# Column mean of an 8192 x 8192 matrix: the first load in two halves, the early load in mid-stream, the last groups loaded in pairs

## The chip, the cores and the metric

The kernel runs on one core of a Trainium2 chip. The metric is device time in microseconds (us) for one execution; the time shown for a kernel is the median of several runs. A profile is one execution taken by the hardware profiler. Its engines are called PE (TensorE), DVE (VectorE), ACT (ScalarE), POOL (GpSimd) and SP (SyncE, which here issues the loads).

## The reference

```python
def setup_inputs():
    return {"x": np.random.randn(8192, 8192).astype(np.float32)}

def reference(x: np.ndarray) -> np.ndarray:
    return np.mean(x, axis=0)
```

256 MiB of float32 (268.4 MB) are read once, and 8192 column means are written.

## The kernel before

The 8192 rows are cut into 64 groups of 128 rows (G = 64), numbered 0 to 63; one group is 128 partitions x 8192 columns, 4 MB. A block is F = 512 columns, so a group has 16 blocks. The tile `bufs` holds six such groups: four slots for loads (0 to 3), `both` (slot 4) and the accumulator `acc` (slot 5).

*Loads.* All loads are issued by SP, in program order, through `load` (line 76). A load into a slot waits for the VectorE add that last read the slot. `load_rows` loads n adjacent groups at once, with partition p taking n adjacent rows; the sum over rows is the same. The order is: the last two blocks of group 60 into `early` (0.5 MB); groups 0 to 3 in one load of 16 MB; groups 4 and 5 straight into `both` and `acc`; five blocks (9 to 13) of group 63 into `early` (1.25 MB); then from group 6 to group 55 pairs of 8 MB, each into two of the four slots in turn; then single groups 56 to 59, 14 blocks of group 60, groups 61 and 62, and group 63 in four pieces (blocks 4 to 7, 0 to 3, 14 and 15, 8).

*Adds.* `add` (line 96) makes a VectorE addition. Where it waits for a load and for the add before it, a no-op on ScalarE or GpSimd waits for both (line 99) and VectorE waits for the no-op. The first two adds fold groups 0 to 3 and then 4 and 5 in a width of 16384 columns. In the loop every pair costs two adds, `both = a + b` and `acc = acc + both`; the first of them frees the pair's slots. At groups 24 and 32 GpSimd adds parts of `early` into `acc` (line 129), 4 blocks and 3. Groups 56 to 59 cost one add each. Of group 60 VectorE adds blocks 0 to 13, of group 61 blocks 7 to 15. GpSimd adds blocks 14, 15 and 8 of group 62 (line 148).

*The end.* What is left is summed over partitions by TensorE with a matrix whose entries are 1/8192 (line 183), into PSUM tiles `bank` (blocks 0 to 7), `wide` (blocks 9 to 13), `two` (14, 15) and `last` (8). TensorE takes its matmuls in the order in which the list `sums` was filled: blocks 2 to 4 and 0 to 1 of `acc`, blocks 0 to 6 of group 61, blocks 5 to 7 of `acc`, then groups 62 and 63 as they come, with the rest of `acc` between. Each matmul of 512 columns stands in the trace as two. ScalarE copies the four larger results out of PSUM (line 198), VectorE copies the last one (line 214), and SP and ScalarE issue five small stores (line 201).

Everything around the change stands in program order on SP, ScalarE, GpSimd and TensorE; VectorE's adds run in the order written.

Of the kernel before, what the change touches and what calls it, by code (L numbers as in the profile page):

```python
# [9 lines left out]
def kernel(  # L10
# [2 lines left out]
    x: bass.AP,  # L13
    out: bass.AP,
):

    nc = tc.nc
    f32 = mybir.dt.float32
    M, N = x.shape  # L40
    P = nc.NUM_PARTITIONS
    F = 512
    W = F // 4
    G = M // P
# [3 lines left out]
    sb = ctx.enter_context(tc.tile_pool(name="sb", bufs=1))  # L48
    psp = ctx.enter_context(tc.tile_pool(name="psum", bufs=1, space=bass.MemoryType.PSUM))

    bufs = sb.tile([P, U, N], f32, name="bufs")
    both = bufs[:, U - 2, :]
    acc = bufs[:, U - 1, :]
    ones = sb.tile([P, 32], f32, name="ones")
    early = sb.tile([P, 7 * F], f32, name="early")
    tail = sb.tile([P, W], f32, name="tail")
    warm = sb.tile([P, 32], f32, name="warm")
    nc.gpsimd.memset(ones[:], 1.0 / M)  # L58
# [16 lines left out]
    def load(dst, src):  # L75
        ins = tc.keep_in_program_order(nc.sync.dma_start(out=dst, in_=src)).ins  # L76
        k = len(loads)
        over = loads[k - 8:k - 6] if k >= 8 and k % 2 == 0 else []
        tc.declare_no_dep(ins, group="loads", keep=over, reason="the reader of the buffer waited")
        for o in over:  # L80
            tc.add_manual_dep(ins, o.name, sync, reason="covers the next load too")
        tc.add_to_no_dep_group("loads", ins)
        loads.append(ins)
        return ins

    def rows(g, n=1):
        return x[g * P:(g + n) * P, :]

    def load_rows(g, u, n):
        return load(bufs[:, u:u + n, :], rows(g, n).rearrange("(p j) c -> p j c", j=n))  # L90

    adds, joins = [], {}

    def add(dst, a, b, dmas):

        ins = nc.vector.tensor_add(out=dst, in0=a, in1=b).ins  # L96
        if dmas and adds:
            waiter = nc.scalar if len(adds) % 8 > 1 else nc.gpsimd
            nop = joins[waiter] = tc.keep_in_program_order(waiter.nop()).ins  # L99
            for o in dmas + adds[-1:]:  # L100
                tc.add_manual_dep(nop, o.name, sync, reason="the no-op waits")
            for group in ("loads", "adds"):
                tc.declare_no_dep(ins, group=group, reason="the no-op waited")
            tc.add_manual_dep(ins, nop.name, sync, reason="waits for both at once")
        elif adds:
            tc.declare_no_dep(ins, group="loads", reason="the add ahead waited")
        tc.declare_no_dep(ins, group="early", reason="the no-op waited, or the add behind it")
        tc.add_to_no_dep_group("adds", ins)
        adds.append(ins)

    load(early[:, 5 * F:], rows(G - 4)[:, 14 * F:])
    first, second = load_rows(0, 0, 4), load_rows(4, 4, 2)
    load(early[:, :5 * F], rows(G - 1)[:, 9 * F:14 * F])
    add(bufs[:, 2:4, :], bufs[:, 2:4, :], bufs[:, 0:2, :], [first])
    add(bufs[:, 4:6, :], bufs[:, 4:6, :], bufs[:, 2:4, :], [second])
    add(acc, acc, both, [])
    tc.keep_in_program_order(nc.scalar.copy(out=warm[:], in_=ones[:]))  # L117
    ahead = []
    g = 6
    while g < G - 8:  # L120
        u = (g + 2) % 4
        dma = load_rows(g, u, 2)
        add(both, bufs[:, u, :], bufs[:, u + 1, :], [dma])
        add(acc, acc, both, ahead)
        ahead = []
        if g in (24, 32):
            lo, hi = (0, 4) if g == 24 else (4, 7)
            cols = slice((9 + lo) * F, (9 + hi) * F)
            ins = tc.keep_in_program_order(nc.gpsimd.tensor_add(  # L129
                out=acc[:, cols], in0=acc[:, cols], in1=early[:, lo * F:hi * F])).ins  # L130
            tc.add_to_no_dep_group("early", ins)
            ahead = [ins]
        g += 2

    while g < G - 4:
        row = bufs[:, (g + 2) % 4, :]
        add(acc, acc, row, [load(row, rows(g))])
        g += 1
    for lo, hi, loaded in [(0, 14, 14), (7, 16, 16)]:
        row = bufs[:, (g + 2) % 4, :]  # L140
        dma = load(row[:, :loaded * F], rows(g)[:, :loaded * F])
        cols = slice(lo * F, hi * F)
        add(acc[:, cols], acc[:, cols], row[:, cols], [dma])
        g += 1
    r61, r62, r63 = [bufs[:, (g + 1 + j) % 4, :] for j in range(3)]
    load(r62, rows(g))
    for cols in [slice(14 * F, 16 * F), slice(8 * F, 9 * F)]:
        joined = tc.keep_in_program_order(nc.gpsimd.tensor_add(  # L148
# [7 lines left out]
    def blocks(row, lo, hi):  # L156
        for i in range(lo, hi):
            sums.append((banks[i // 4], i % 4, 0, row[:, i * F:(i + 1) * F]))
# [5 lines left out]
                at = lo * F + q * n + c  # L164
                sums.append((dst, q, c, row[:, at:at + min(F, n - c)]))

    blocks(acc, 2, 5)
    blocks(acc, 0, 2)
    blocks(r61, 0, 7)
    blocks(acc, 5, 8)  # L170
    blocks(r62, 0, 8)
    spread(wide, acc, 9, 14, slice(1))
    blocks(r63, 4, 8)
# [83 lines left out]
```

## Time and profile before

| | |
|---|---|
| Median of 3 runs | 628.53 us (628.39 to 628.57) |
| Span of the profiled execution | 626.4 us |
| VectorE busy | 529.3 us (85%), 60 instructions |
| TensorE busy | 13.3 us (2%), 126 matmuls |
| GpSimd busy | 12.0 us (2%) |
| ScalarE busy | 3.7 us (1%) |
| Read from HBM | 268.44 MB, 429 GB/s over the span |

The profiled execution's span is what the engines and queues cover between its first and last instruction; the time of a run also has what lies around it. Times inside the profile are in us from the start of the span. The chain of waits is followed back from the last instruction to what released it; the timeline merges like instructions that follow each other; the groups give the busy time and the mean of one instruction for each line, engine, operation and shape. In the timeline, the bracket behind a group names how long its engine was idle before it and what ended the idle time.

### The profile page before, as it was taken

Reading aid. Unit: us, or ns where it says so; the run is one execution under the profiler, and the core shown is the slowest. Engines: PE = TensorE matmul, PEld = TensorE weight load, DVE = VectorE, ACT = ScalarE, POOL = GpSimd, SP = SyncE. Lnnn points to the kernel's source line nnn. Section 1 sums busy time; section 2 is a strip of 40 time slices with the busy share of each in tenths; the row PEclk is TensorE's granted clock in tenths of the full one; section 3 lists DMA queues with packets and bytes.
Section 4 is the critical chain, followed back from the end, with each engine's and each line's share of the span. In section 5 each row is a group of like instructions: output and inputs, shape, how many; then the busy total and the mean of one; then the engine's idle time right before and its main releaser. Section 6 shows DMA issues by size and latency. Waiting matters only on the chain.

```text
span 626.4 us, 484 instructions
## 1 busy us (share of the span) xinstructions
PE 13.3 (2%) x126; PEld 4.0 (1%) x126; DVE 529.3 (85%) x60; ACT 3.7 (1%) x6; POOL 12.0 (2%) x10
## 2 busy tenths in 40 slices
PE   0000000000000000000000000000000000000008
PEld 0000000000000000000000000000000000000002
DVE  0028999998888998889998899888898888999992
ACT  0000000000000000000000000000000000000001
POOL 0000000000000000020000200000000000000002
PEclk9999999999999999999999999999999999999999
DMA  8999999999999999999999999999999999999997
GB/s 372 465 402 428 459 410 460 402 469 402 469 402 469 402 469 402 469 402 469 402 465 406 439 431 427 444 410 460 402 469 402 469 402 469 402 435 435 419 435 305
DMA packets 5930, 268.50 MB, mean 429 GB/s; under 512 B 660, under 2 KB 668, under 8 KB 1064
## 3 DMA queue, kind: packets, MB, share of 16 engines
q1 hardware_dynamic: 5912, 268.46, 99.3%
q8 instruction: 1, 0.02, 0.0%
q10 hardware_dynamic: 16, 0.01, 0.0%
q14 instruction: 1, 0.01, 0.0%
HBM read 268.44 MB, written 0.03 MB: 429 GB/s over the span
## 4 chain that ended last, share of the span: by engine, by line
DMA 59%; DVE 30%; another core or an unknown queue 10%; issue 0%; SPq 0%; ACTq 0%; PE 0%; POOL 0%; POOLq 0%
DMA bufs<-in_x_dram 59%; DVE bufs L96 30%; SPq L76 0%; ACTq L99 0%; PE last L183 0%; DVE tail L214 0%; POOL ready L61 0%; POOL ones L58 0%; POOLq L99 0%; POOLq L241 0%
## 5 line engine op out<-in xcount | busy, mean ns | idle before, releaser
L96 DVE TENSOR_TENSOR bufs<-bufs 128x8192 f32<-128x8192 f32 (+3 forms) x59 | 529.0, 8966 | 85.9 <-DMA bufs<-in_x_dram 43.0
L183 PE MATMUL bank<-bufs,ones 128*32 128x512 f32 x62 | 10.0, 716 | 610.3 <-DVE bufs L96 610.0
L129 POOL TENSOR_TENSOR bufs<-bufs,early 128x2048 f32<-128x2048 f32 (+1 forms) x2 | 7.9, 3954 | 348.5 <-DVE bufs L96 348.5
L148 POOL TENSOR_TENSOR bufs<-bufs 128x1024 f32<-128x1024 f32 (+1 forms) x2 | 3.6, 1824 | 258.9 <-DMA bufs<-in_x_dram 258.9
L214 DVE COPY tail<-last 128x128 f32<-128x128 f32 x1 | 0.3, 291 | 8.8 <-PE last L183 8.8
L183 PEld LDWEIGHTS bank<-bufs,ones 128*32 128x32 f32 x62 | 2.2, 121 | 616.4 <-issue 614.5
L198 ACT COPY bufs<-bank 128x512 f32<-128x512 f32 x2 | 1.2, 586 | 617.9 <-PE bank L183 617.9
L183 PE MATMUL wide<-bufs,ones 128*32 128x512 f32 (+1 forms) x32 | 2.5, 432 | 0.0
L117 ACT ACT_TABLE_LOAD x1 | 1.3, 1283 | 0.7 <-PEq L241 0.7
L183 PE MATMUL two<-bufs,ones 128*32 128x256 f32 x16 | 1.2, 380 | 0.0
L183 PEld LDWEIGHTS wide<-bufs,ones 128*32 128x32 f32 x32 | 1.0, 110 | 1.8 <-issue 1.8
L183 PE MATMUL last<-bufs,ones 128*32 128x128 f32 x16 | 0.8, 279 | 0.1
L198 ACT COPY bufs<-wide 128x640 f32<-128x640 f32 x1 | 0.7, 692 | 1.1 <-PE wide L183 1.1
L183 PEld LDWEIGHTS last<-bufs,ones 128*32 128x32 f32 x16 | 0.4, 109 | 1.2 <-issue 0.6
L183 PEld LDWEIGHTS two<-bufs,ones 128*32 128x32 f32 x16 | 0.4, 109 | 0.1
L198 ACT COPY bufs<-two 128x256 f32<-128x256 f32 x1 | 0.4, 372 | 0.1
L117 ACT COPY warm<-ones 128x32 f32<-128x32 f32 x1 | 0.2, 217 | 0.0
L61 POOL TENSOR_TENSOR ready<-ones 128x1 f32<-128x1 f32 x1 | 0.2, 193 | 0.1
L58 POOL MEMSET ones<- 128x32 f32 x1 | 0.1, 125 | 0.3 <-POOLq L241 0.3
L241 POOL MEMSET const-float32-0.0<- 128x1 f32 x1 | 0.1, 98 | 0.2 <-issue 0.2
L241 POOL MEMSET const-bfloat16-1.0<- 128x1 bf16 x1 | 0.1, 102 | 0.0
L241 POOL MEMSET const-uint8-127<- 128x1 uint8 x1 | 0.1, 102 | 0.0
(1 smaller groups left out, 0.1 us busy)
## 6 DMA issues: line engine op xcount, KB each, us to landing
bufs<-in_x_dram SPq DMA_DIRECT2D x6, 4096.0 KB, 20.4
bufs<-in_x_dram SPq DMA_DIRECT2D x1, 3584.0 KB
bufs<-in_x_dram SPq DMA_DIRECT2D x2, 1024.0 KB, 18.7
early<-in_x_dram SPq DMA_DIRECT2D x1, 1280.0 KB
early<-in_x_dram SPq DMA_DIRECT2D x1, 512.0 KB
bufs<-in_x_dram SPq DMA_DIRECT2D x1, 512.0 KB, 19.4
bufs<-in_x_dram SPq DMA_DIRECT2D x27, 29.9
bufs<-in_x_dram SPq DMA_DIRECT2D x1, 256.0 KB, 19.7
```

Source lines behind the costliest of these rows:

```text
L58: nc.gpsimd.memset(ones[:], 1.0 / M)
L61: nc.gpsimd.tensor_add(out=ready[:], in0=ones[:, 0:1], in1=ones[:, 1:2]))
L96: ins = nc.vector.tensor_add(out=dst, in0=a, in1=b).ins
L117: tc.keep_in_program_order(nc.scalar.copy(out=warm[:], in_=ones[:]))
L129: ins = tc.keep_in_program_order(nc.gpsimd.tensor_add(out=acc[:, cols], in0=acc[:, cols], in1=early[:, lo * F:hi * F])).ins
L148: joined = tc.keep_in_program_order(nc.gpsimd.tensor_add(out=acc[:, cols], in0=acc[:, cols], in1=r62[:, cols])).ins
L183: summed = tc.keep_in_program_order(nc.tensor.matmul(out=dst[32 * q:32 * q + 32, c:c + cols.shape[1]], lhsT=ones[:], rhs=cols, start=all(( ...
L198: return tc.keep_in_program_order(nc.scalar.copy(out=dst, in_=src)).ins
L214: ended = nc.vector.tensor_copy(out=tail[:], in_=last[:]).ins
L241: nc = _bacc.Bacc("TRN2", target_bir_lowering=False, num_devices=1)
```

## The change

The load of groups 0 to 3 becomes two loads of two groups, and the first add waits for both through a no-op (the condition in `add` lets the first add do so). The load of two blocks of group 60 into `early` goes. The load of five blocks of group 63 into `early` is issued behind the load of group 12 instead of behind the loads at the start. The loop of pairs runs to group 59 instead of 55. Groups 60 and 61 are loaded as one pair, group 60 with all 16 blocks. VectorE adds group 60 whole to `acc` and then blocks 7 to 15 of group 61. GpSimd's two adds from `early` take 3 blocks and 2. TensorE's list begins with blocks 0 to 6 of group 61, followed by blocks 0 to 7 of `acc`; the rest of the list is the same.

```diff
-    early = sb.tile([P, 7 * F], f32, name="early")
+    early = sb.tile([P, 5 * F], f32, name="early")
...
-        if dmas and adds:
+        if dmas and (adds or len(dmas) > 1):
...
-    load(early[:, 5 * F:], rows(G - 4)[:, 14 * F:])
-    first, second = load_rows(0, 0, 4), load_rows(4, 4, 2)
-    load(early[:, :5 * F], rows(G - 1)[:, 9 * F:14 * F])
-    add(bufs[:, 2:4, :], bufs[:, 2:4, :], bufs[:, 0:2, :], [first])
-    add(bufs[:, 4:6, :], bufs[:, 4:6, :], bufs[:, 2:4, :], [second])
+    dmas = [load_rows(g, g, 2) for g in (0, 2, 4)]
+    add(bufs[:, 2:4, :], bufs[:, 2:4, :], bufs[:, 0:2, :], dmas[:2])
+    add(bufs[:, 4:6, :], bufs[:, 4:6, :], bufs[:, 2:4, :], dmas[2:])
...
-    while g < G - 8:
+    while g < G - 4:
         u = (g + 2) % 4
         dma = load_rows(g, u, 2)
+        if g == 12:
+            load(early[:], rows(G - 1)[:, 9 * F:14 * F])
...
-            lo, hi = (0, 4) if g == 24 else (4, 7)
+            lo, hi = (0, 3) if g == 24 else (3, 5)
...
-    while g < G - 4:
-        row = bufs[:, (g + 2) % 4, :]
-        add(acc, acc, row, [load(row, rows(g))])
-        g += 1
-    for lo, hi, loaded in [(0, 14, 14), (7, 16, 16)]:
-        row = bufs[:, (g + 2) % 4, :]
-        dma = load(row[:, :loaded * F], rows(g)[:, :loaded * F])
-        cols = slice(lo * F, hi * F)
-        add(acc[:, cols], acc[:, cols], row[:, cols], [dma])
-        g += 1
-    r61, r62, r63 = [bufs[:, (g + 1 + j) % 4, :] for j in range(3)]
+    u = (g + 2) % 4
+    dma = load_rows(g, u, 2)
+    add(acc, acc, bufs[:, u, :], [dma])
+    r61 = bufs[:, u + 1, :]
+    add(acc[:, 7 * F:], acc[:, 7 * F:], r61[:, 7 * F:], [])
+    g += 2
+    r62, r63 = [bufs[:, (g + 2 + j) % 4, :] for j in range(2)]
...
-    blocks(acc, 2, 5)
-    blocks(acc, 0, 2)
     blocks(r61, 0, 7)
-    blocks(acc, 5, 8)
+    blocks(acc, 0, 8)
     blocks(r62, 0, 8)
```

## The prediction, made before the changed kernel ran

> **What bounds the kernel now.** I read the page first (engines, queues, chain), then the chain of waits in order of time, then the timeline of the last 20 us, then the groups by form for durations, and last the windows of the transfer rate.
>
> ```profile
> span 626.4 us, 484 instructions
> q1 hardware_dynamic: 5912, 268.46, 99.3%
> ```
>
> The loads' queue is busy for 99.3% of the span, 622.0 us. No engine's arithmetic fills the span (VectorE 85%). So bytes set the pace up to the tail. The rate by windows (columns: stretch, busy times, clock, DMA share, GB/s):
>
> ```profile
> 61.50:64.00 2.50, 0.00 (x0) 0.00 (x0) 1.59 (x1) 0.00 (x0) 0.00 (x0) 1.00 0.96 360
> 470.40:509.10 38.70, 0.00 (x0) 0.00 (x0) 34.77 (x4) 0.00 (x0) 0.00 (x0) 1.00 1.00 434
> 549.40:606.40 57.00, 0.00 (x0) 0.00 (x0) 56.34 (x7) 0.00 (x0) 0.00 (x0) 1.00 1.00 432
> ```
>
> The reader sees 434 GB/s with paired loads, 432 with single ones, and 360 while `early` streams near 62 us. Four groups take 38.70 us, one group 9.67. The chain of waits in time (start, length, what):
>
> ```profile
> 1.13 61.22 another core or an unknown queue
> ...
> 593.41 8.70 DVE bufs L96
> ...
> 603.45 19.74 DMA bufs<-in_x_dram
> 623.19 0.04 issue
> 623.23 0.47 PE last L183 x8
> 623.73 0.29 DVE tail L214
> ```
>
> It ends on the last piece of group 63, as if VectorE and TensorE had room. The timeline of the tail shows how little room TensorE has:
>
> ```profile
> 609.98 6.01 PE L183 MATMUL bank<-bufs,ones 128*32 128x512 f32 x30 [609.98 <-DVE bufs L96]
> 611.71 0.20 PEld L183 LDWEIGHTS bank<-bufs,ones 128*32 128x32 f32 x7 [0.68 <-issue]
> 612.56 0.18 PEld L183 LDWEIGHTS bank<-bufs,ones 128*32 128x32 f32 x1 [0.66 <-issue]
> 613.41 0.16 PEld L183 LDWEIGHTS bank<-bufs,ones 128*32 128x32 f32 x5 [0.68 <-issue]
> 613.88 0.12 PEld L183 LDWEIGHTS bank<-bufs,ones 128*32 128x32 f32 x3 [0.31 <-issue]
> 614.31 0.12 PEld L183 LDWEIGHTS bank<-bufs,ones 128*32 128x32 f32 x3 [0.31 <-issue]
> 614.95 0.14 PEld L183 LDWEIGHTS bank<-bufs,ones 128*32 128x32 f32 x2 [0.52 <-DVE bufs L96]
> 616.28 0.16 PEld L183 LDWEIGHTS bank<-bufs,ones 128*32 128x32 f32 x8 [1.19 <-DMA bufs<-in_x_dram]
> ...
> 618.02 1.04 PE L183 MATMUL wide<-bufs,ones 128*32 128x512 f32 x8
> ...
> 618.88 1.04 PE L183 MATMUL bank<-bufs,ones 128*32 128x512 f32 x8
> ...
> 622.54 0.62 PE L183 MATMUL two<-bufs,ones 128*32 128x256 f32 x8
> ```
>
> Group 62 lands at about 616.25. From 616.28 TensorE runs group after group without a hole: 1.74 us for group 62's eight blocks of 512 (616.28 to 618.02), 0.86 for four (618.02 to 618.88), and so on. After `two` at 622.54 comes its second half, to 622.97; the final group then waits until 623.23. The slack of that stream is 0.26 us in 7. VectorE's last add ends just before 614.95, 1.3 us ahead of group 62. The page's clock column stays at full, but the rhythm of the weight loads halves at 613.41, from 0.85 to 0.43 us, 3.43 us after TensorE's first matmul. I read this as its clock rising: 0.43 us a block before, 0.217 after.
>
> **The change, part by part.** The sum is made against the span, 626.4; the median of 628.53 lies 2.1 above it, and I add that at the end.
>
> *Groups 60 and 61 as one load.* Bytes ahead of group 62 are the same, so apart from the stream term below the pair lands when group 61 does now: 616.25 - 9.67 = 606.58. But group 60 now arrives with it; it used to land 9.7 us earlier and was added by then. Both adds now come after the landing:
>
> ```profile
> L96 DVE TENSOR_TENSOR bufs<-bufs 128x4608 f32<-128x4608 f32 x1 | 5.0, 4957 | 0.1
> ```
>
> No-op and start 0.06 (as 549.44 to 549.50 in the chain), group 60 whole 8.70, a gap of 0.02, half of 61 at 4.96: VectorE ends at 620.32, 5.4 us later than now. It is free in time for this: group 58's pair lands 19.35 earlier at 587.2, and its two adds, 17.4, end at 604.7.
>
> What is queued behind that add? TensorE takes its matmuls in order: group 61's seven blocks at 606.6, `acc`'s blocks 0 to 6 at 615.4, then block 7 of `acc`, which needs the second add, and behind it everything of groups 62 and 63, landed or not. So the stream that begins at 616.28 now begins at 620.37. It needs 0.22 for block 7 and the 6.69 that lie between 616.28 and 622.97: the last group starts at 627.28 instead of 623.23, **+4.05**. All of 63 has landed by then. GpSimd waits for the same add: its two (2.37 and 1.28, after 0.2 to start) end by 624.2, and TensorE asks for them after 625; hidden by 1 us. ScalarE's copies and the stores follow TensorE as they do now and shift with it.
>
> *TensorE's clock.* The early bursts are now apart: seven blocks at 606.6 (3.0 us at the slow rate), nothing until 615.4, seven blocks until 618.4, nothing until 620.37. Bounds from the row of 3.43 us: 0 if the burst before the hole counts and the clock is up by 620.4; 6.9 if it never rises, which doubles the stream of 6.9. If the count starts afresh at 620.37, 3.43 us at half speed cost 1.7; if one such stretch is missed, 3.4. The burst of 3.0 is only 0.4 short of the 3.43, so I can't decide between about 0 and 1.7 and take the middle, **+0.9**; 3.4 is the end that I keep for the range.
>
> [...]
>
> *Single loads 56 to 61 as pairs.* 57 us at 432 against 434 GB/s: -0.26. Their waits for VectorE are hidden: the pair 60 waits only for the first add of 56, done some 10 us before the transfers ahead run out; likewise 62 and 63 behind 58.
>
> *The load of four groups as two of two; `early` moved and cut to 5 blocks.* The first add still waits for four groups, now over a GpSimd no-op (0.05). The small load ahead of them goes, its bytes return in group 60. First bytes move between 1.5 and 2.0 us; 17.3 MB at 434 GB/s need 39.9, so 41.4 to 41.9, and VectorE starts at 42.99: at most 0.5 of that excess can go. The 360 GB/s while `early` streams cost 0.43 in 2.5 us, which may or may not return in mid-stream. Gains 0 to 0.9.
>
> Against this, `early` was the cover of one issue. The load of group 6 waits for the first add, 17.23 long, and is issued at 60.25; groups 4 and 5 land at 62.35, and behind them `early` keeps the queue busy to 65. Without it the queue must get new bytes before 62.35 less the lag from last byte to landing, about 0.6 (the rate falls off at 622.6, the last landing is 623.2). At the start, 0.74 from the issue, bytes move after 0.8 to 1.3: 61.05 to 61.55 against 61.75. Cover remains by 0.2 to 0.7, and once more near 79 for the load of group 8; from there VectorE's two adds of 17.4 gain on 19.35. Bounds 0 and 0.5 lost; I take 0.25. [...]
>
> In all the stream term is -0.26 - 0.2 + 0.25, **-0.2**, ends -1.2 and +0.3. The smaller GpSimd adds at 24 and 32 (3 and 2 blocks for 4 and 3) shorten only adds of VectorE that end far before the next landing; nothing.
>
> **Sum.** 626.4 + 4.05 + 0.9 - 0.2 = 631.15 of span, and 2.1 around it: 633.3 us. A measurement can tell 0.2% from no change, 1.3 us; this is +4.8.
>
> **Rivals.**
>
> *The clock falls behind for longer* (windows that begin without regard to the work): +2.6 to +3.4 in place of 0.9, 635 to 636. For it: the two bursts are split by holes of 5 and 2 us. Against: the one rise that the trace has came just as 3.43 us of work were full.
>
> *The first add's issue comes too late.* If new bytes need 1 us more than at the start, both early places stall, the second less since everything ahead moves back too: about +1.2 on the sum, 634.5. Against it: the start itself is 1.3 at most.
>
> *The end stays with the last load* (the other side). The chain gives the last 19.74 us to transfers; VectorE's 5.4 us would vanish in slack, and with the stream's -0.2 the time would be 628.3, with -1.2 it would be 627.3. This decides if what follows VectorE's end needs less than 623.2 - 620.4 = 2.8 us. It needs 6.9 at the fast rate. Even if the whole overhead of the stream went, 622.0 less 268.46 MB at 434 GB/s, 3.4 us, the end would still be 0.65 late.
>
> *The change doesn't do what it says.* If TensorE could take group 62 ahead of block 7, 1.74 of the 4.05 would go: 631.6. The order of the matmuls is fixed in the text, with `acc` 0 to 8 ahead of it, so this is unlikely.
>
> **Chances.** Forecast (TensorE's stream starts 4 us late, clock costs up to 1.7) 0.60; clock longer 0.24; late issue 0.07; matmuls overtaking 0.04; end with the load 0.05. Slower by over 0.2%: 0.95; of the last 0.05, 0.03 within and 0.02 faster. Range: clock 0 with -0.6 of the stream gives 631.7, clock 3.4 with -0.2 gives 635.8, with +0.1 some 636.1: 631.7 to 636.0.
>
> **What would show it.** VectorE's last add ending near 620 and TensorE's eight blocks of group 62 starting just behind it, not behind a landing; the chain ending on VectorE and TensorE instead of the 19.74 us of DMA; weight loads 0.86 apart (slow) or 0.43 after 620. It is wrong if group 62's matmuls start at its landing, if the pair lands more than 1 us off 606.6, or if holes in the transfers show near 61 and 79.

## The result, and the profile after

| | before | after |
|---|---|---|
| Median of 4 runs | 628.55 us (628.39 to 628.81) | 636.97 us (636.38 to 637.62) |
| Span of the profiled execution | 626.4 us | 634.9 us |
| Queue of the loads, share of the span | 99.3% | 98.0% |

The changed kernel takes 1.0136 times as long, interval 1.0123 to 1.0149: 8.4 us slower. The prediction was 633.3 with a range of 631.7 to 636.0; the direction and the mechanism held, the size did not.

The page of the changed kernel:

```profile
span 634.9 us, 474 instructions
PEclk9999999999999999999999999999999999999997
q1 hardware_dynamic: 5352, 268.46, 98.0%
```

The loads' queue was busy for 98.0% of a longer span, 622.2 us, as long as before: the 8.5 us are time in which it had nothing to do, most of it behind the last load (its landing, by the semaphore in the trace, came at 623.19 before and 624.68 after, so 3.2 us of the span followed it before and 10.2 after). The last digit of the clock row is 7 now, where before it was 9: TensorE had less than its full clock in the last slice.

The end of the chain of waits after (start, length, what):

```profile
578.19 29.92 DMA bufs<-in_x_dram
608.11 0.04 POOLq L77
608.15 0.02 issue
608.17 8.70 DVE bufs L74
616.88 0.02 issue
616.90 4.97 DVE bufs L74
621.87 0.04 issue
621.91 4.43 PE bank L155 x17
626.35 0.06 PE wide L155 x3
626.40 0.37 PE bank L155
626.77 0.43 PE wide L155 x4
...
631.73 0.23 PE last L155 x2
631.96 0.02 issue
631.98 0.29 DVE tail L186
```

Before, this chain ended with 19.74 us of transfers and 0.47 us of matmuls. Now it leaves the transfers at 608.11, when groups 60 and 61 land together, and runs over VectorE's two adds, and then over TensorE for 10.1 us. The timeline of the tail after (start, length, what, idle time before it):

```profile
608.25 3.63 PE L155 MATMUL bank<-bufs,ones 128*32 128x512 f32 x14 [608.25 <-DMA bufs<-in_x_dram]
...
616.92 3.63 PE L155 MATMUL bank<-bufs,ones 128*32 128x512 f32 x14 [5.04 <-DVE bufs L74]
...
621.91 4.43 PE L155 MATMUL bank<-bufs,ones 128*32 128x512 f32 x17 [1.36 <-DVE bufs L74]
621.94 3.59 POOL L122 TENSOR_TENSOR bufs<-bufs 128x1024 f32<-128x1024 f32 x2 [264.84 <-DVE bufs L74]
622.77 0.29 PEld L155 LDWEIGHTS bank<-bufs,ones 128*32 128x32 f32 x4 [0.56 <-issue]
623.62 0.29 PEld L155 LDWEIGHTS bank<-bufs,ones 128*32 128x32 f32 x4 [0.56 <-issue]
...
626.61 0.11 PEld L155 LDWEIGHTS wide<-bufs,ones 128*32 128x32 f32 x1 [0.26 <-issue]
```

TensorE stands three times, and each time VectorE or the landing of the pair releases it. After 621.91 the weight loads stand 0.85 us apart, and near 626.6 the gap before them falls from 0.56 to 0.26: the slow rhythm first, then the fast one. The mean granted clock of this execution is 0.992; the trace's record of the clock has it at half for 10.24 us (615.93 to 626.17), which gives that.

The 8.5 us between the two spans, read from these lines and those of before:

| Step | before | after | difference |
|---|---|---|---|
| Group 61 has landed | 606.5 | 608.1 | 1.6 |
| From there to the start of TensorE's last stream | 9.8 | 13.8 | 4.0 |
| From there to VectorE's last copy | 7.45 (616.28 to 623.73) | 10.07 (621.91 to 631.98) | 2.6 |
| From there to the end | 2.66 | 2.92 | 0.3 |

(606.5 before is the landing's semaphore in the trace. The last stream begins with group 62 before, and after with block 7 of `acc`, which stands ahead of group 62.) The second row is the predicted mechanism. The first and the third are what the experiments are about.

### The profile page after: what moved, and what is told of

Same layout as the page of the kernel before. It is cut to its first block, busy times and chain, and to the rows that moved or that the text cites. A ratio compares the mean times of both kernels' runs of the same rounds, so it can differ in the third digit from the quotient of the medians.

```text
span 634.9 us, 474 instructions
## 1 busy us (share of the span) xinstructions
PE 17.3 (3%) x126; PEld 5.8 (1%) x126; DVE 528.2 (83%) x60; ACT 3.7 (1%) x6; POOL 9.9 (2%) x10
## 4 chain that ended last, share of the span: by engine, by line
DMA 68%; DVE 27%; another core or an unknown queue 3%; PE 2%; issue 0%; SPq 0%; POOLq 0%; ACTq 0%
DMA bufs<-in_x_dram 68%; DVE bufs L74 27%; PE bank L155 1%; PE wide L155 0%; PE two L155 0%; PE last L155 0%; SPq L54 0%; POOLq L77 0%; ACTq L77 0%; DVE tail L186 0%
## 5 line engine op out<-in xcount | busy, mean ns | idle before, releaser
L74 DVE TENSOR_TENSOR bufs<-bufs 128x8192 f32<-128x8192 f32 (+2 forms) x59 | 527.9, 8948 | 93.9 <-POOLq L77 54.8
L155 PE MATMUL bank<-bufs,ones 128*32 128x512 f32 x62 | 15.3, 930 | 614.6 <-DMA bufs<-in_x_dram 608.2
L107 POOL TENSOR_TENSOR bufs<-bufs,early 128x1536 f32<-128x1536 f32 (+1 forms) x2 | 5.8, 2877 | 350.2 <-DVE bufs L74 350.2
L186 DVE COPY tail<-last 128x128 f32<-128x128 f32 x1 | 0.3, 292 | 10.1 <-PE last L155 10.1
L170 ACT COPY bufs<-bank 128x512 f32<-128x512 f32 x2 | 1.2, 586 | 626.4 <-PE bank L155 626.4
L155 PE MATMUL wide<-bufs,ones 128*32 128x512 f32 (+1 forms) x32 | 4.4, 468 | 0.0
```

The source lines that it names most:

```text
L107: ins = tc.keep_in_program_order(nc.gpsimd.tensor_add(out=acc[:, cols], in0=acc[:, cols], in1=early[:, lo * F:hi * F])).ins
L155: summed = tc.keep_in_program_order(nc.tensor.matmul(out=dst[32 * q:32 * q + 32, c:c + cols.shape[1]], lhsT=ones[:], rhs=cols, start=all(( ...
L170: return tc.keep_in_program_order(nc.scalar.copy(out=dst, in_=src)).ins
L186: ended = nc.vector.tensor_copy(out=tail[:], in_=last[:]).ins
```

## The experiments

All times are medians; the kernel before ran beside them at 628.3 to 628.5.

### Where the first 1.6 us come from

**cover_back** puts the early load of 1.25 MB back behind the loads of groups 0 to 5, in the changed kernel.

```diff
     dmas = [load_rows(g, g, 2) for g in (0, 2, 4)]
+    load(early[:], rows(G - 1)[:, 9 * F:14 * F])
...
-        if g == 12:
-            load(early[:], rows(G - 1)[:, 9 * F:14 * F])
```

> Changed kernel with the early load of 1.25 MB back behind the loads of groups 0 to 5. Theory (the queue runs dry when the load of group 6 is issued late without cover): groups 60 and 61 land near 606.5 instead of 608.1, no loss in the landings of groups 6 and 8, time 1.6 us under the changed kernel, about 635.4, give or take 0.7 for the clock's phase. Rival (the split first load or the paired last loads themselves cost the 1.6): landing stays at 608.1, time stays at 637.0.

Measured: 633.02 (632.80 to 633.25), 3.95 under the changed kernel, more than expected. The chain of its profile, span 630.9:

```profile
606.23 0.04 POOLq L77
606.27 0.02 issue
606.30 8.70 DVE bufs L74
615.00 0.02 issue
615.02 4.97 DVE bufs L74
619.99 0.04 issue
620.03 2.33 PE bank L154 x17
```

The pair lands at 606.23 instead of 608.11, so the loss lies in the start and has nothing to do with the paired loads at the end. The other 2.1 us are in the last line: the same 17 matmul records that took 4.43 us take 2.33. TensorE's clock was up in this execution before VectorE was done: the trace's record of the clock has it rise at 619.38, against 626.17 in the changed kernel. In the changed kernel it was thus at half for the first 4.26 us of the last stream, and half of that is 2.1.

**start_alone** is the other half: the kernel before with the changed start alone.

```diff
-    load(early[:, 5 * F:], rows(G - 4)[:, 14 * F:])
-    first, second = load_rows(0, 0, 4), load_rows(4, 4, 2)
-    load(early[:, :5 * F], rows(G - 1)[:, 9 * F:14 * F])
+    dmas = [load_rows(g, g, 2) for g in (0, 2, 4)]
...
         dma = load_rows(g, u, 2)
+        if g == 12:
+            load(early[:, 5 * F:], rows(G - 4)[:, 14 * F:])
+            load(early[:, :5 * F], rows(G - 1)[:, 9 * F:14 * F])
```

> Kernel before with only the start of the change: three loads of two groups, and both early loads behind the load of group 12. Theory (stream loses about 2.1 us at the issues of groups 6 and 8, gains 0.3 where early streams): every later landing about 1.7 us later and the end with it, about 630.2. Rival (in a kernel whose end is the last load, VectorE's slack or the stream takes the loss back): 628.5.

Measured: 630.59 (630.20 to 631.69), ratio 1.0038, interval 1.0023 to 1.0053. Its chain has the landing of groups 54 and 55 at

```profile
551.94 0.04 ACTq L99
551.98 0.02 issue
552.00 8.70 DVE bufs L96
```

where before it was at 549.44, with the same bytes ahead of it. The loss stays in the stream until the end: the span is 628.9 us, 2.5 above that of before.

Where in the start? Windows of the changed kernel (stretch, busy times, clock, DMA share, GB/s):

```profile
1.50:4.50 3.00, 0.00 (x0) 0.00 (x0) 0.00 (x0) 0.73 (x2) 0.00 (x0) 1.00 1.05 350
60.50:63.50 3.00, 0.00 (x0) 0.00 (x0) 2.20 (x1) 0.00 (x0) 0.00 (x0) 1.00 1.00 350
470.40:509.10 38.70, 0.00 (x0) 0.00 (x0) 34.77 (x5) 0.00 (x0) 0.00 (x0) 1.00 1.00 434
```

The three microseconds from 60.5 look like the three with which the program begins: the queue had run empty on most of its sixteen streams and started again. In the trace's records of single transfers the streams end their old work between 60.55 and 60.88 and begin the new between 60.71 and 61.80, 1.5 to 2.6 us after the issue. Up to eleven of them stand still at once, and the first 64 KB on each then take 2.6 to 3.5 us instead of 2.42. The load of group 6 was issued at 59.20 and the loads ahead of it landed at 61.24; it landed at 82.10 instead of 61.24 + 19.35 = 80.59, and the load of group 8 lost 0.55 more.

**cover_part** gives a part of the cover back: two of the five early blocks (0.5 MB) at the start, three behind group 12.

```diff
     dmas = [load_rows(g, g, 2) for g in (0, 2, 4)]
+    load(early[:, :2 * F], rows(G - 1)[:, 9 * F:11 * F])
...
-            load(early[:], rows(G - 1)[:, 9 * F:14 * F])
+            load(early[:, 2 * F:], rows(G - 1)[:, 11 * F:14 * F])
```

> Changed kernel with two of the five early blocks (0.5 MB, 1.2 us of the queue) behind the loads of groups 0 to 5, the other three behind the load of group 12. Theory (the load of group 6 needs some 2 to 4 us more of lead than it has): the loss in the landing of group 6, 1.5 to 3.7 us without cover and none with 3.0 us of cover, falls by about the 1.2 of the cover, to 0.3 to 2.5; time near 635. Rival (any small load ahead of it removes the loss): 633.0, as with the whole early load.

Measured: 634.19 (634.04 to 636.07). By the landings in the trace the load of group 6 loses 0.8 us against the landing of the small load, which itself comes 0.4 late, so about 1.2 in all. Over all profiled executions the loss at groups 6 and 8 was 2.1, 2.1, 2.8 and 3.7 us without cover (the changed kernel, start_alone, singles, filler), 1.2 with 1.2 us of cover, and with 3.0 us of cover at most 0.2 at group 6 in eight profiled executions; in three of these 0.4 to 0.5 us went in all at groups 6 to 12, and why is open. Of the four runs of cover_part three lie at 634.04 to 634.23 with a mean granted clock of 1.000 and one at 636.07 with 0.992. These 1.9 us fit a cost of the clock, but the slow run was not the profiled one, so where its clock was down is not seen.

### What TensorE's clock costs

**filler** leaves the changed kernel as it is and keeps TensorE busy: 30 matmuls into a tile that nothing reads.

```diff
     blocks(r61, 0, 7)
-    blocks(acc, 0, 8)
+    fill(20)
+    blocks(acc, 0, 7)
+    fill(10)
+    blocks(acc, 7, 8)
     blocks(r62, 0, 8)
```

> Changed kernel with 30 matmuls more on TensorE, of a block of group 61 into a PSUM tile that nothing reads: 20 behind group 61's blocks, 10 behind acc's blocks 0 to 6, all before VectorE's last add ends. Theory (TensorE's clock is down from VectorE's end at 621.9 for 4 us): weight loads 0.43 apart from 621.9 on, time about 2.0 us under the changed kernel, 635.0. Rival (the clock doesn't matter, the order of the blocks or the stores do): 637.0 or more.

Measured: 635.96 (635.38 to 636.79), 1.0 under the changed kernel, half of what was expected. The chain shows why the medians hide it:

```profile
610.16 0.04 POOLq L77
...
618.95 4.97 DVE bufs L74
623.92 0.04 issue
623.97 2.33 PE bank L164 x17
...
631.94 0.29 DVE tail L195
```

In this execution the start had lost 3.7 us and the pair landed at 610.16. From the start of TensorE's stream to VectorE's copy it took 7.97 us (623.97 to 631.94), against 10.07 in the changed kernel: 2.1 us are the clock. The loss at the start varies from run to run by more than a microsecond, so a difference of medians is no measure of the clock here; the stretch from TensorE's start to the copy is.

**cover_filler** has the same 30 matmuls in cover_back, where the start loses little.

> The kernel with the early load back as cover (633.02 when measured, stretches of slow clock in two of its four runs, but none of them behind VectorE's last add in the profiled one), with the 30 matmuls that nothing reads. Theory (the clock costs time only where it is down behind VectorE's last add): 8.0 us from VectorE's end to the last copy, as in the profiled run with cover, time 632.9, at most 0.3 under 633.02. Rival (the slow clock before VectorE's end costs time too): 632.0 or less.

Measured: 633.08 (632.83 to 633.25), no difference to 633.02, with 7.97 us from TensorE's start to the copy again (620.40 to 628.37). In cover_back the clock was down from 612.55 to 619.38, all of it ahead of VectorE's end at 619.99, and this cost nothing against cover_filler. Filler matmuls are a test here and no cure.

Why was the clock down in the changed kernel and up in cover_back, with the same bursts in the same distances? In the trace's record of the clock, changes stand 3.413 us apart or a multiple of it, and these marks lie differently against the kernel in each execution. In the changed kernel the clock rose at 612.52, fell at 615.93, and rose again at 626.17, behind the stretch from 622.76, the first that was full of matmuls. In cover_back it rose at 619.38: there the burst of 3.63 us from 615.04 filled 79% of one stretch, while in the changed kernel it filled 71% of one and left 60% to the next. The measured cost of 2.1 us lies between two of the prediction's cases, a count that starts afresh at 620.37 (1.7) and one stretch more that is missed (3.4). In these two runs the clock rose behind a stretch that was 79% busy and not behind one of 71%.

### What VectorE's late end costs

**singles** loads and adds groups 56 to 61 one by one in the changed kernel.

```diff
-    while g < G - 4:
+    while g < G - 8:
...
-    u = (g + 2) % 4
-    dma = load_rows(g, u, 2)
-    add(acc, acc, bufs[:, u, :], [dma])
-    r61 = bufs[:, u + 1, :]
-    add(acc[:, 7 * F:], acc[:, 7 * F:], r61[:, 7 * F:], [])
-    g += 2
+    while g < G - 3:
+        row = bufs[:, (g + 2) % 4, :]
+        add(acc, acc, row, [load(row, rows(g))])
+        g += 1
+    r61 = bufs[:, (g + 2) % 4, :]
+    add(acc[:, 7 * F:], acc[:, 7 * F:], r61[:, 7 * F:], [load(r61, rows(g))])
+    g += 1
```

> Changed kernel with groups 56 to 61 loaded one by one and added one by one (group 60 still whole, 61 half, start as changed). Theory (VectorE's late end is made by the landing in pairs): VectorE's last add ends near 616.5, before group 62 lands at 617.8; TensorE's group 62 starts at that landing; time about 630.2, which is the time of before plus the loss at the start. Rival (group 60 whole and the new order of acc's blocks cost as much): 633 or more.

Measured: 631.71 (630.93 to 632.00), 1.5 over the expectation. In the profile VectorE ends at 617.47 and group 62 lands at 618.97, so VectorE is done before the landing, as expected. The start lost 2.8 us in this execution, and the clock was down from 617.44 to 620.85, while group 62 came in.

**cover_singles** is the same with the early load back at the start. Of the change there remain the split first load, group 60 whole, and the new order of `acc`'s blocks.

> Kernel with cover, with groups 56 to 61 loaded and added singly. Theory (nothing else of the change costs time): VectorE ends near 614.7, before group 62 lands at 616, time 628.4 as before the change, plus up to 0.9 if TensorE's clock falls in the hole before group 62. Rival (a further cost in group 60 whole or in acc's order): 630 or more.

Measured: 628.54 over ten runs, ratio 1.0011, interval 1.0001 to 1.0021. VectorE ends at 615.00, and in the chain group 62's matmuls again wait for their landing:

```profile
592.37 24.15 DMA bufs<-in_x_dram
616.52 0.04 issue
616.56 1.92 PE bank L155 x16
```

Six runs lie at 628.2 to 628.6 with a mean clock of 1.000, four at 629.2 to 630.3 with 0.997. So the tail in pairs costs 633.02 - 628.54 = 4.5 us. The 3.95 us between the changed kernel and cover_back are the loss at the start and the 2.1 us of the clock, and what remains of the change costs 0.2 us by the medians, with the four runs at a mean clock of 0.997 among the ten.

**cover_single60** keeps pairs up to 59 and loads only 60 and 61 singly (the second part of the diff of singles, in cover_back).

> Kernel with cover, with groups 60 and 61 loaded and added singly, 56 to 59 still in pairs. Theory (VectorE is busy with the pair 58 until 604.4, so group 60's add can start only 1.9 us earlier than with the pair 60): VectorE ends near 618.1 instead of 620.0, time 631.1 if the clock is up. Rival (only the common landing of 60 and 61 matters): VectorE ends near 615, time 628.5.

Measured: 632.09 (631.34 to 633.16). VectorE ends at 618.34, near the 618.1 of the theory and far from 615: the pair 58 keeps it busy until 604.5, so undoing the last pair alone gives back 1.6 of the 5 us. The two runs with a mean clock of 0.997 take 631.3 and 631.6, the two with 1.000 take 632.6 and 633.2. The profiled one is of the first kind and has its clock up from 617.24; what made the others longer is not seen (a mean of 1.000 does not exclude a slow stretch ahead of the first rise, see the end).

**cover_order62** lets TensorE take group 62 ahead of block 7 of `acc`, in cover_back.

```diff
-    blocks(acc, 0, 8)
-    blocks(r62, 0, 8)
+    blocks(acc, 0, 7)
+    blocks(r62, 0, 8)
+    blocks(acc, 7, 8)
```

> Kernel with cover, and TensorE takes group 62's eight blocks ahead of block 7 of acc. Theory (TensorE's queue stands behind block 7): of the 8.0 us behind VectorE's last add the 1.74 of group 62 go ahead of it, time 631.2. Rival (the path runs through GpSimd's adds or the copies behind VectorE's end): 632.7 or more.

Measured: 631.19 (630.98 to 631.43), 1.8 less. Its chain no longer has VectorE's second add:

```profile
606.46 8.70 DVE bufs L74
...
615.21 6.12 PE bank L155 x32
621.32 0.86 PE wide L155 x8
...
626.57 0.29 DVE tail L186
```

TensorE's stream, which starts with `acc` at 615.21, now ends the kernel by itself. The order of the queue is worth those 1.8 us; VectorE's lateness still sets the 615.21. The clock was down until 620.24 in this execution, so slow matmuls are a part of the 6.12 us.

### A version that might beat both, and two runs for its spread

**cover_singles_fill** adds ten idle matmuls to cover_singles, six ahead of `acc`'s block 7 and four behind it, to hold the clock up until group 62.

```diff
-    blocks(acc, 0, 8)
+    blocks(acc, 0, 7)
+    fill(6)
+    blocks(acc, 7, 8)
+    fill(4)
     blocks(r62, 0, 8)
```

> Kernel with cover and single loads from group 56 on, with ten matmuls that nothing reads in TensorE's hole before group 62. Theory (the slow runs of that kernel, 630.1 with a mean clock of 0.997, had the clock fall in this hole): no run above 629, median 628.3, no different from before the change at 628.4. Rival (those runs have another cause): some runs at 630 again.

Measured: 628.71 over eleven runs (628.44 to 630.89), ratio 1.0016, interval 1.0006 to 1.0026. It doesn't beat the kernel before, and four runs lie at 630.2 to 630.9, two of them with a mean clock of 1.000. The theory fell for these. **fill_again** is a second profile of this kernel, **singles_again** one of cover_singles.

> The kernel with cover, single loads and ten idle matmuls once more, for a profile of a run near 630.6, of which it had four in eleven. Theory (the stream lost about 2 us near the issues of groups 6 to 12): in such a run group 62 lands near 618.7. Rival (TensorE is late though its clock is up): group 62 lands near 616.6 and its matmuls start later. A run near 628.5 tells nothing of it.

> The kernel with cover and single loads once more, for a profile of a run near 630.1 with a mean clock of 0.997, of which it had four in ten. Theory (TensorE's clock falls in the hole before group 62): group 62 lands near 616.5 as in the run of 628.6, the weight loads behind it stand 0.86 apart for up to 3.4 us, and the end is 1.7 later. Rival: group 62 lands later. A run near 628.4 tells nothing of it.

Both caught such a run. singles_again (629.39, clock 0.997) has group 62 landing at 616.24 as usual, and its timeline is

```profile
614.82 4.46 PE L155 MATMUL bank<-bufs,ones 128*32 128x512 f32 x18 [2.20 <-DVE bufs L74]
```

where cover_singles had group 62's sixteen records alone in 1.92 us. The clock fell at 614.87, behind a hole of 2.2 us, and rose at 618.28, as the theory had it; but the span is only 0.7 us longer than in the profile of cover_singles, and not the 1.7 expected. fill_again (630.78, clock 1.000) meets neither theory nor rival: group 62 landed on time at 616.48 and TensorE followed with the fast rhythm. Its windows near the end:

```profile
622.50:623.00 0.50, 0.50 (x16) 0.35 (x11) 0.00 (x0) 0.34 (x2) 0.00 (x0) 1.00 0.45 144
623.00:623.50 0.50, 0.50 (x10) 0.13 (x2) 0.00 (x0) 0.50 (x1) 0.00 (x0) 1.00 0.00 0
624.50:625.00 0.50, 0.10 (x4) 0.10 (x8) 0.00 (x0) 0.00 (x0) 0.00 (x0) 1.00 0.05 16
```

The last bytes of group 63 had moved by 623.0, yet the last matmuls start only at 624.9, with the landing. Fifteen of the sixteen marks of that landing stood by 623.4 and one came at 624.86. The records of single transfers suggest a cause: a transfer of 16 KB of the kind "instruction", on queue 8, ran from 622.68 to 623.77, and the write of the late mark stands at 623.76, where the other fifteen had been written by 622.90. Every profiled execution has such a transfer, of 0.9 to 1.3 us, between 622 and 630, but in no other does a mark stand at its end. The records don't name the engine that carried a transfer, so that the mark waited behind this one is not shown. It would explain 0.9 of the 1.5 us. Whether the other runs above 630 have the same cause is open.

## Why the prediction was right or wrong, point by point

*The pair makes VectorE late and TensorE later: right.* From the landing of the pair to the end of VectorE's adds the prediction had 13.74 us, the profile has 13.76. TensorE stood at block 7 as forecast and took up its stream 0.04 us behind VectorE, so the signs that the prediction named for this came true. cover_order62 shows the queue's order at work, singles and cover_singles that VectorE leaves the path when the groups land one by one, cover_single60 that the pair 58 had its part in it. This last point was said in the prediction only as a cover (its adds "end at 604.7"); it also means that there was no short way back.

*The stream: wrong, and this is the step that failed.* The term was -0.2 with ends -1.2 and +0.3; measured it is +1.6. Within it the issue of group 6's load without cover was put at 0.25 with a bound of 0.5. The landings show 2.1 us lost at groups 6 and 8, and 0.4 or so gained elsewhere in the stream. Two of the prediction's signs of being wrong came true: the pair landed at 608.1, 1.5 us off 606.6, and the transfers have a hole near 61. The working set the time from an issue until bytes begin to move (0.8 to 1.3) against the time until the queue is empty. The records have 1.5 to 2.6 us for the first, while the streams ran out 1.35 to 1.7 us after the issue, and the first transfers were slow besides (2.6 to 3.5 us for 64 KB, 2.42 otherwise). A safer measure is the whole time that a load takes beyond its bytes. The profile of before had that number: from the first issue at 0.74 to the landing of the first four groups at 42.97 are 42.2 us, of which 39.9 are bytes (17.3 MB with the small load ahead) at 434 GB/s, so 2.4 us are extra. The prediction had seen a part of it (VectorE starting at 42.99 where the bytes alone end at 41.4 to 41.9) and did not carry it to the late issue. Against a lead of 2.1 us, from the issue at 60.25 to the landing at 62.35, it says that no cover is left, but only 0.3 us of loss. The measured loss was larger: from the issue of group 6 to its landing are 22.9 us for 8 MB, where the first 8 MB of the changed kernel took 21.8. Why the late issue costs more than the first one, and 1.5 to 3.7 us from one execution to the next, is open. The rival of the late issue had the right place and a price of 1.2, and got a chance of 0.07.

*TensorE's clock: mechanism right, size off.* The term was 0.9, the middle between a burst that counts and one that doesn't; measured 2.1 (10.07 against 7.97 us). The rival with a longer wait for the clock (2.6 to 3.4 in place of 0.9) was nearer. What the prediction held against it, a rise just 3.43 us after the first matmul, was chance: in the kernel before the stretch of 3.413 us that ended with the rise (at 613.47) began 0.08 us behind that matmul, while in start_alone, with the same matmuls, the rise came 4.5 us after the first (612.48 to 616.96). In these runs the cost went with where the marks of the clock fell (2.1 us in the changed kernel, none in cover_back), so it is a spread and no constant. How often the bad case comes is not known: the mean clock was 0.992 in all four runs of the changed kernel, and in none of cover_back's four.

*Block 7 of `acc`: 0.22 forecast, less 0.26 of wait.* With the clock up, TensorE's stream takes 7.97 us instead of 7.45, 0.5 more where about nothing was expected. The chain after shows matmuls of `bank` and `wide` mixed in ones and threes, where before there were whole groups of four or eight; that a lone block ahead puts the groups of four out of step is the author's guess. In cover_order62, where block 7 comes behind eight others, the chain has whole groups again. That the mixing costs the 0.5 is not shown; no run tries it by itself.

*Pairs instead of singles in the stream, the split first load, the smaller GpSimd adds: right.* cover_back lands group 61 at 606.23, 0.3 ahead of before, near the -0.26, and cover_singles stands 0.1% above before.

Summed by the prediction's own terms: 4.05 became 4.5 (4.0 of it VectorE, 0.5 block 7), 0.9 became 2.1, -0.2 became 1.6, and 0.3 behind the last copy, which no run explains, came to it: 8.5. The forecast of the same steps was 4.75.

## What to carry to other kernels

A queue that is 99% busy can still depend on one small transfer that covers a late issue: here 1.25 MB, and the load behind it landed 1.5 us late without them. Before such a transfer is moved, compare the lead of the next issue (issue to the landing of what is ahead; here 2.1 us) with what a whole load takes beyond its bytes (here 2.4 at the start and more at the late issue), not with the time to its first byte. Joining the last loads gained 0.3 us of the stream here and cost 4 behind the last landing; and with short bursts of matmuls (3.6 us) and holes between them (5.0 and 1.4 us) the clock was down right where the changed kernel ends, at a cost of 2.1 us, and up there in cover_back.

## What the runs showed of the hardware that was not expected

- A load of 8 MB issued 2.0 us ahead of the end of the queue lost 1.5 to 3.7 us, differently in each execution; one issued 5.1 us ahead (with 3.0 us of cover) lost at most 0.2.
- TensorE's clock rose after a stretch of 3.413 us that was 79% busy and not after one of 71%, nor in cover_singles_fill after one of 75% (the stretch up to 609.63); in singles and singles_again it fell behind stretches busy for some 35%, and in cover_singles it stayed up through one of 47%. These shares are worked out from the matmuls' modelled ends.
- The mean granted clock doesn't tell of a slow stretch ahead of the first rise: cover_filler shows 1.000, and its first matmuls have the slow rhythm.
- Of the sixteen marks of one landing, one came 1.5 us behind the others, written just as a 16 KB instruction transfer ended (fill_again).
